# Weight sums tied in order to the score products, and spread over eight steps a group

## The chip, the cores and the metric

The kernel runs on one core of one Trainium2 chip. The metric is the device time of one execution in microseconds (us), lower is better. Engines: PE is TensorE, DVE is VectorE, ACT is ScalarE, POOL is GpSimd, and SP is the engine whose queue issues all the DMAs of this kernel.

## The reference

One decoder layer on 1024 tokens of width 1024. The normed input is projected; a gated linear recurrence with 4 heads and a causal attention with 8 heads of 64 run on parts of the projection; their outputs are merged by gates; then come a gated feed-forward network of width 2816 and a gated embedding. What matters here is the attention and the last product of the feed-forward network:

```python
s = jnp.einsum('bhtd,bhsd->bhts', qh[:, :, t0:t1], kh[:, :, :t1]) * scale
s = s + c[:, :, t0:t1, None] - c[:, :, None, :t1]
s = jnp.where(mask, s, -jnp.inf)
pr = jax.nn.softmax(s, axis=-1).astype(vh.dtype)
outs.append(jnp.einsum('bhts,bhsd->bhtd', pr, vh[:, :, :t1]))
...
x = x + (jax.nn.silu(hf @ w_ffn_gate[layer]) * (hf @ w_ffn_up[layer])) @ w_ffn_down[layer]
```

## The kernel before, in words

Every product of the projections is done as three products of numbers split into a high and a low part (`mm3`, lines 153 to 158, and lines 402 to 404 in `nproj`).

The last product of the feed-forward network is done by a scheme with seven block products instead of eight. It needs four sums of blocks of the weights for each of 11 pairs of row groups. These sums depend on nothing but the weights. `down_sums` (lines 775 to 794) makes them early, during the attention: for each pair, a "group", it loads four blocks of 128x512 (line 781), makes four sums in place on POOL (lines 783, 785, 788, 791) and stores each to DRAM (lines 786, 789, 792, 794), from where they are loaded much later. The tiles come from a pool of six buffers. `down_sums` is a generator, and each `next(wsums, None)` at line 870 runs one step of it, up to the next `yield`. A group takes five steps; the store of its last sum falls into the first step of the next group.

The attention runs in four passes, one for each pair of heads (`fox_mix`, line 847). A pass places the pair's q and k by DMA (`fox_place`, tiles QA, KA, QB, KB) and its values (`fox_values`, tiles VH, VL), and then has two parts. The first finds the largest score of each query: 24 products (line 862, for 16 of them with a mask product at line 865), each followed by a reduction on DVE (line 867), one step of the weight sums (line 870) and 0.6 step of other work (`fill(0.6)`). The maxima are transposed (line 875), split into uh and ul on DVE (lines 878, 879) and put by four DMAs into rows 66 and 67 of QA (line 882). The second part, the weighing, makes the scores again with these rows (lines 908, 909), takes the exponential on ACT (line 915), rounds it on POOL (line 919), makes the rest on DVE (line 920) and multiplies with the values (lines 896 to 898).

The work that `fill` takes is the stream of the pass: passes 0 and 1 have a projection of the attention (`fox_project`, 32 steps; it has a small power on POOL, line 661, and stores to DRAM, line 669) and two projections of gates (16 steps each, `gate_spill`, stored at line 684); pass 2 has three of the gates; pass 3 has one and three more that aren't stored. A pass fills 10 steps ahead of its first product, 14.4 beside the products, 5 ahead of the transposes and 9 behind them, and drains what is left at its end.

PE's order is that of the program (`manual_schedule`). The other engines' queues, SP's and POOL's among them, are ordered when the kernel is compiled: an instruction that the compiler takes to be ready can be put ahead of an earlier one that it takes not to be. Each queue then runs in that order, and waits where an operand isn't there yet.

Of the kernel before, what the change touches and what calls it, by code (L numbers as in the profile page):

```python
# [14 lines left out]
ALU = mybir.AluOpType  # L15
# [4 lines left out]
P = 128  # L20
# [3 lines left out]
HALF = 512  # L24
# [20 lines left out]
U_DOWN = U_UP + NFF  # L45
# [18 lines left out]
def layer(ctx, tc, xT, pT, wts, wf_in, consts, masks, outT):  # L64
    nc = tc.nc
    dma = nc.sync.dma_start
# [3 lines left out]
    ptt = nc.gpsimd.tensor_tensor  # L70
    pts = nc.gpsimd.tensor_scalar
    mm = nc.tensor.matmul
# [59 lines left out]
    order = [8, 9, 10, 11, 4, 0, 24, 25, 26, 27]  # L132
# [5 lines left out]
    for n, m in GATES_BEFORE:  # L138
        i = order.index(n)
# [145 lines left out]
    for c in range(8):  # L285
        t = w2() if c < 4 else hg.tile([P, HALF], F32, tag=("Kt", "Qt")[c % 2], name="vraw")
# [9 lines left out]
    identb = const.tile([P, P], BF, name="identb")  # L296
    nc.vector.tensor_copy(identb, ident)
    mnat = const.tile([P, P], BF, name="mnat")
# [394 lines left out]
    for i, (u, t) in enumerate(tiles):  # L693
        hi, lo = weight(u)
        for h in range(2):
            ps = zbank() if len(banks) < 3 else mbank()
# [60 lines left out]
    QA = [fx.tile([P, T], R, tag=f"QA{i}", bufs=1, name="QA") for i in range(2)]  # L757
    KA = [fx.tile([P, T], R, tag=f"KA{i}", bufs=1, name="KA") for i in range(2)]
# [12 lines left out]
    sd = dram.tile([4, NPAIR, P, HALF], F32, name="sd")  # L771
    wsum = fstack.enter_context(tc.tile_pool(name="wsum", bufs=6, reuse_waits="tile"))
    S2, S3, S4, S1 = range(4)

    def down_sums():

        for kp in range(NPAIR):
            t = {}
            for n, (i, b) in (("21", (0, 1)), ("22", (1, 1)), ("11", (0, 0)), ("12", (1, 0))):
                t[n] = wsum.tile([P, HALF], F32, tag="sw", name="sw")  # L780
                dma(t[n], wts[U_DOWN + 2 * kp + i][:, b * HALF:(b + 1) * HALF])
            yield
            ptt(t["22"], t["21"], t["22"], ALU.add)
            yield
            ptt(t["21"], t["11"], t["21"], ALU.subtract)
            dma(sd[S1, kp], t["22"])
            yield
            ptt(t["11"], t["22"], t["11"], ALU.subtract)
            dma(sd[S3, kp], t["21"])
            yield  # L790
            ptt(t["12"], t["12"], t["11"], ALU.subtract)
            dma(sd[S2, kp], t["11"])
            yield
            dma(sd[S4, kp], t["12"])

    wsums = down_sums()
    staged = {}

# [21 lines left out]
    def fox_place(pr):  # L820

        qhi, qlo = staged.pop((pr, 0))
        khi, klo = staged.pop((pr, 1))
        for a in range(2):
            s = slice(a * 64, a * 64 + 64)
            hd = pr * 2 + a
            dma(fb(QA[a][0:64]), fb(qhi[s]))
            dma(fb(KA[a][0:64]), fb(khi[s]))
            dma(fb(KA[a][64:65]), crow[hd:hd + 1])
            dma(fb(KA[a][65:66]), crow[8 + hd:9 + hd])  # L830
        for a in range(2):
            s = slice(a * 64, a * 64 + 64)
            dma(fb(QB[a][0:64]), fb(qlo[s]))
            dma(fb(QB[a][64:128]), fb(qhi[s]))
            dma(fb(KB[a][0:64]), fb(khi[s]))
            dma(fb(KB[a][64:128]), fb(klo[s]))
# [10 lines left out]
    def fox_mix(pr, steps, before):  # L847
        fox_place(pr)
        fox_values(pr)
        fill(10)  # L850

        u = const.tile([P, 16], F32, tag="u", name="u")
        u2 = const.tile([P, 8], F32, tag="u2", name="u2")
        for a in range(2):
            for b in range(8):
                tb = slice(b * P, (b + 1) * P)
                for g in range(1 if b < 4 else 2):
                    s1 = min((g + 1) * HALF, (b + 1) * P)
                    n = s1 - g * HALF
                    ps = mbank()  # L860
                    diag = s1 == (b + 1) * P and (b < 4 or g == 1)
                    mm(ps[:, 0:n], QA[a][0:66, tb], KA[a][0:66, g * HALF:s1], start=True,  # L862
                       stop=not diag)
                    if diag:
                        mm(ps[:, n - P:n], identb, mnat, start=False, stop=True)
                    dst = u[:, a * 8 + b:a * 8 + b + 1] if g == 0 else u2[:, a * 4 + b - 4:a * 4 + b - 3]
                    nc.vector.tensor_reduce(dst, ps[:, 0:n], axis=AX.X, op=ALU.max, negate=True)
                    if before:
                        before.pop(0)()
                    next(wsums, None)  # L870
                    fill(0.6)
            tt(u[:, a * 8 + 4:a * 8 + 8], u[:, a * 8 + 4:a * 8 + 8], u2[:, a * 4:a * 4 + 4], ALU.min)
        fill(5)
        pu = mbank()
        nc.tensor.transpose(pu[0:16, 0:P], u, ident)
        uh = fx.tile([16, P], R, tag="uh", bufs=1, name="uh")
        ul = fx.tile([16, P], R, tag="ul", bufs=1, name="ul")
        nc.vector.tensor_copy(uh, pu[0:16, 0:P])
        tt(ul, pu[0:16, 0:P], fb(uh), ALU.subtract)
        for a in range(2):  # L880
            for i, t in enumerate((uh, ul)):
                dma(fb(QA[a][66 + i:67 + i]), fb(t[a * 8:a * 8 + 8]))
        fill(9)
        LAG = 3
        HEAD = 0
        count = 0
        late = []
        for h in range(2):
            av = [abank(), abank()]
            nblk = 4 * (h + 1)  # L890
            pend = []

            def weigh():
                i, a, off, n, ph, pl = pend.pop(0)
                vs = slice(i * 192 + a * 64, i * 192 + a * 64 + P)
                mm(av[a][:, off:], VH[:, vs], ph[:, 0:n], start=i == 0, stop=False)
                mm(av[a][:, off:], VL[:, vs], ph[:, 0:n], start=False, stop=False)
                mm(av[a][:, off:], VH[:, vs], pl[:, 0:n], start=False, stop=i == nblk - 1)

            for i in range(nblk):  # L900
                t0 = max(i * P, h * HALF)
                t1 = (h + 1) * HALF
                n = t1 - t0
                sb = slice(i * P, (i + 1) * P)
                for a in range(2):
                    ps = mbank()
                    diag = i * P >= h * HALF
                    mm(ps[:, 0:n], KA[a][0:68, sb], QA[a][0:68, t0:t1], start=True, stop=False)  # L908
                    mm(ps[:, 0:n], KB[a][:, sb], QB[a][:, t0:t1], start=False, stop=not diag)
                    if diag:  # L910
                        mm(ps[:, 0:P], identb, mtr, start=False, stop=True)  # L911
                    p = fx.tile([P, HALF], F32, tag="p", bufs=2, name="p")
                    ph = fx.tile([P, HALF], R, tag="ph", bufs=3, name="ph")
                    pl = fx.tile([P, HALF], R, tag="pl", bufs=3, name="pl")
                    act(p[:, 0:n], ps[:, 0:n], AF.Exp)  # L915
                    if count < HEAD:
                        act(ph[:, 0:n], ps[:, 0:n], AF.Exp)
                    else:
                        pts(ph[:, 0:n], p[:, 0:n], 1.0, 0.0, ALU.mult, ALU.add)  # L919
                    tt(pl[:, 0:n], p[:, 0:n], fb(ph[:, 0:n]), ALU.subtract)  # L920
                    pend.append((i, a, t0 - h * HALF, n, ph, pl))
                    fill(0.87)
                    if len(pend) >= LAG:
                        weigh()
                    count += 1
                    if count in steps:
                        steps[count]()
                    if late and count % 2:
                        late.pop(0)()
            while pend:  # L930
                weigh()
                fill(0.87)
            den = f2()
            y = f2()
            nc.vector.tensor_copy(den[0:64], av[0][64:128])
            nc.vector.tensor_copy(den[64:128], av[1][0:64])
            nc.scalar.copy(y[0:64], av[0][0:64])
            nc.scalar.copy(y[64:128], av[1][64:128])

            def divide(q, h=h, den=den, y=y):  # L940
                s = slice(q * P, (q + 1) * P)
                nc.vector.reciprocal(den[:, s], den[:, s])
                tt(y[:, s], y[:, s], den[:, s], ALU.mult)
                if q == 3:
                    dma(yb[pr * P:(pr + 1) * P, h * HALF:(h + 1) * HALF], y)

            late += [lambda q=q, f=divide: f(q) for q in range(4)]
        return late
# [111 lines left out]
    op = ostack.enter_context(tc.tile_pool(name="op", bufs=3, side="right", reuse_waits="tile"))  # L1060
# [267 lines left out]
    for n, (p, kp) in enumerate(todo):  # L1328
# [22 lines left out]
        _, _, g, begin, into, done = products[p]  # L1351
# [129 lines left out]
```

## Time and profile before

| | us |
|---|---|
| median of 3 runs (lowest, highest) | 1703.51 (1701.68, 1705.78) |
| profiled execution | 1703.0 |
| its span | 1701.2 |
| PE busy | 1620.6 (95%) |
| DVE busy | 1097.1 (64%) |
| ACT busy | 639.1 (38%) |
| POOL busy | 600.0 (35%) |

The span runs from the first to the last instruction of the profiled execution; its own time has 1.8 us more. Busy is the time in which an engine executes; the rest of the span it waits or has nothing to do. The mean granted clock of PE is 0.98 of full.

### The profile page before, as it was taken

To read this page: it belongs to the slowest core of one execution; us is meant where nothing else is said; L and a number is where in the kernel's file an instruction comes from. 1 tells how busy PE (TensorE), PEld (TensorE's weight loads), DVE (VectorE), ACT (ScalarE), POOL (GpSimd) and SP (SyncE) were. 2 spreads that over 40 slices of the span, in tenths; PEclk is the share of its full clock that TensorE was granted. 3 is DMA by queue.
4 is the path that set the end of the run, shared out by engine and by line. 5 is a ranking of instruction groups with operands and counts; after the bars stand their busy time and mean duration, and the time that the engine had idled before them with its cause. 6 is when DMAs were issued, how large, how long until landed. Compare 5 with 4: busy or idle time off the path is not lost.

```text
span 1701.2 us, 21473 instructions
## 1 busy us (share of the span) xinstructions
PE 1620.6 (95%) x8086; PEld 1356.7 (80%) x8086; DVE 1097.1 (64%) x1431; ACT 639.1 (38%) x888; POOL 600.0 (35%) x452
## 2 busy tenths in 40 slices
PE   8999999998289799999999999999999999999998
PEld 7889889997168577777888888888888878888887
DVE  7457776755066566666557777777777757666442
ACT  7244645632032214357224433332333334444310
POOL 2343454423572503021213466566656620111200
PEclk9999999999599899999999999999999999999999
DMA  5332121245665653517134322233223278665111
GB/s 205 100 112 75 65 72 51 87 135 162 234 242 144 216 135 99 138 44 278 50 134 144 113 99 94 96 121 114 97 93 115 81 277 288 196 188 186 62 68 44
DMA packets 120615, 223.45 MB, mean 131 GB/s; under 512 B 14368, under 2 KB 43424, under 8 KB 120512
## 3 DMA queue, kind: packets, MB, share of 16 engines
q1 hardware_dynamic: 120512, 222.09, 39.7%
q8 instruction: 63, 1.03, 0.3%
q14 instruction: 40, 0.33, 0.1%
HBM read 148.25 MB, written 61.15 MB: 123 GB/s over the span
## 4 chain that ended last, share of the span: by engine, by line
PE 83%; issue 4%; POOL 3%; DMA 3%; DVE 3%; ACT 2%; SPq 1%; POOLq 0%; ACTq 0%; DVEq 0%
PE ps_z L156 14%; PE ps_z L157 14%; PE ps_z L158 14%; PE ps_m L156 6%; PE ps_m L158 6%; PE ps_m L157 6%; PE ps_z L402 2%; PE ps_z L403 2%; PE ps_z L404 2%; DMA sw<-wts 2%; PE ps_m L488 1%; PE ps_a L158 1%; PE ps_a L156 1%; PE ps_a L157 1%; PE ps_m L862 1%
## 5 line engine op out<-in xcount | busy, mean ns | idle before, releaser
L156 PE MATMUL ps_z<-xhi,whi 128*128 128x512 f32 x624 | 254.8, 408 | 0.2 <-ACT xhi L173 0.2
L157 PE MATMUL ps_z<-xlo,whi 128*128 128x512 f32 x624 | 246.0, 394 | 0.6 <-DVE xlo L176 0.5
L158 PE MATMUL ps_z<-xhi,wlo 128*128 128x512 f32 x624 | 245.3, 393 | 0.0
L158 PEld LDWEIGHTS ps_z<-xhi,wlo 128*128 128x128 f32 x624 | 118.3, 190 | 25.2
L1078 DVE TENSOR_TENSOR wlo<-dr,whi 128x1024 fp32r<-128x1024 f32 x75 | 94.9, 1267 | 66.6 <-ACT whi L1077 64.5
L157 PEld LDWEIGHTS ps_z<-xlo,whi 128*128 128x128 f32 x624 | 118.8, 190 | 23.0 <-DVE xlo L176 2.5
L156 PEld LDWEIGHTS ps_z<-xhi,whi 128*128 128x128 f32 x624 | 119.5, 192 | 21.6 <-ACT xhi L173 0.8
L128 ACT CAST whi<-raw 128x1024 fp32r<-128x1024 f32 (+1 forms) x69 | 72.4, 1049 | 169.7 <-PE ps_z L157 120.8
L920 DVE TENSOR_TENSOR pl<-p,ph 128x512 fp32r<-128x512 f32 (+3 forms) x96 | 62.6, 658 | 102.9 <-POOL ph L919 102.6
L1077 ACT CAST whi<-dr 128x1024 fp32r<-128x1024 f32 x75 | 79.1, 1055 | 108.6 <-PE ps_m L158 92.0
L129 DVE TENSOR_TENSOR wlo<-raw,whi 128x1024 fp32r<-128x1024 f32 (+1 forms) x69 | 100.6, 1458 | 29.0 <-ACT whi L128 24.6
L402 PE MATMUL ps_z<-whi,xhi 128*128 128x256 f32 (+1 forms) x384 | 112.8, 294 | 0.0
L919 POOL TENSOR_SCALAR ph<-p 128x512 fp32r<-128x512 f32 (+3 forms) x96 | 55.2, 578 | 157.7 <-ACT p L915 157.3
L403 PE MATMUL ps_z<-wlo,xhi 128*128 128x256 f32 (+1 forms) x384 | 108.6, 283 | 0.0
L404 PE MATMUL ps_z<-whi,xlo 128*128 128x256 f32 (+1 forms) x384 | 108.5, 283 | 0.0
L1271 POOL TENSOR_TENSOR w<-w,rb 128x512 f32<-128x512 f32 x44 | 63.1, 1435 | 103.4 <-ACT w L1270 103.4
L915 ACT ACTIVATE p<-ps_m 128x512 f32<-128x512 f32 (+3 forms) x96 | 46.2, 490 | 132.5 <-PE ps_m L911 92.6
L1300 POOL TENSOR_TENSOR acc<-acc,o 128x512 f32<-128x512 f32 x14 | 24.8, 1770 | 190.5 <-ACT o L1299 189.9
L908 PE MATMUL ps_m<-QA,KA 68*128 68x512 f32 (+3 forms) x96 | 35.0, 364 | 46.2 <-DMA QA<-ul 45.8
L403 PEld LDWEIGHTS ps_z<-wlo,xhi 128*128 128x128 f32 x384 | 73.3, 191 | 0.7
L402 PEld LDWEIGHTS ps_z<-whi,xhi 128*128 128x128 f32 x384 | 73.4, 191 | 0.1
L404 PEld LDWEIGHTS ps_z<-whi,xlo 128*128 128x128 f32 x384 | 73.0, 190 | 0.0
(465 smaller groups left out, 4454.2 us busy)
## 6 DMA issues: line engine op xcount, KB each, us to landing
raw<-wts SPq DMA_DIRECT2D x71, 512.0 KB
hb<-w SPq DMA_DIRECT2D x77, 256.0 KB
dr<-hb SPq DMA_DIRECT2D x75, 256.0 KB
sw<-wts SPq DMA_DIRECT2D x44, 256.0 KB
sd<-sw SPq DMA_DIRECT2D x44, 256.0 KB
rg<-wts SPq DMA_DIRECT2D x22, 512.0 KB
ru<-wts SPq DMA_DIRECT2D x22, 512.0 KB
dr<-sd SPq DMA_DIRECT2D x44, 256.0 KB
```

The lines of the kernel that those rows point to most:

```text
L128: nc.scalar.copy(hi, raw)
L129: tt(lo, raw, hi.bitcast(F32), ALU.subtract)
L156: mm(ps, w[0], x[0], start=first, stop=False, skip_group_check=more)
L157: mm(ps, w[0], x[1], start=False, stop=False, skip_group_check=more)
L158: mm(ps, w[1], x[0], start=False, stop=last, skip_group_check=more)
L402: mm(ps[:, off:off + n], xh[:, cs], hi, start=k == 0, stop=False)
L403: mm(ps[:, off:off + n], xh[:, cs], lo, start=False, stop=False)
L404: mm(ps[:, off:off + n], xl[:, cs], hi, start=False, stop=k == KT - 1)
L920: tt(pl[:, 0:n], p[:, 0:n], fb(ph[:, 0:n]), ALU.subtract)
L1077: nc.scalar.copy(hi, src)
L1078: tt(lo, src, hi.bitcast(F32), ALU.subtract)
L1271: ptt(s, s, hv(rb, h), ALU.mult)
```

## The change

Every load, sum and store of the weight sums gets an edge to the latest product of the largest scores (`anchor[0]`): it is put behind that product in the order made when the kernel is compiled. The edge is one of order alone (`NoSync`), and no wait comes from it. The steps of a group become eight: loads; two empty ones; a sum; then three times the store of the last sum and the next sum; then the last store. The sums and the order among them are the same.

```diff
+    anchor = [None]
+
+    def after_anchor(ins):
+
+        tc.add_manual_dep(ins.ins, anchor[0].ins.name,
+                          mybir.DependencyInfo(mybir.DependencyClass.NoSync,
+                                               mybir.DependencyReason.DATA), reason="order")
+
     def down_sums():
 
         for kp in range(NPAIR):
             t = {}
             for n, (i, b) in (("21", (0, 1)), ("22", (1, 1)), ("11", (0, 0)), ("12", (1, 0))):
                 t[n] = wsum.tile([P, HALF], F32, tag="sw", name="sw")
-                dma(t[n], wts[U_DOWN + 2 * kp + i][:, b * HALF:(b + 1) * HALF])
+                after_anchor(dma(t[n], wts[U_DOWN + 2 * kp + i][:, b * HALF:(b + 1) * HALF]))
             yield
-            ptt(t["22"], t["21"], t["22"], ALU.add)
             yield
-            ptt(t["21"], t["11"], t["21"], ALU.subtract)
-            dma(sd[S1, kp], t["22"])
             yield
-            ptt(t["11"], t["22"], t["11"], ALU.subtract)
-            dma(sd[S3, kp], t["21"])
+            for x, y, z, op, n in (("21", "22", "22", ALU.add, S1), ("11", "21", "21", ALU.subtract, S3),
+                                   ("22", "11", "11", ALU.subtract, S2), ("12", "11", "12", ALU.subtract, S4)):
+                after_anchor(ptt(t[z], t[x], t[y], op))
+                yield
+                after_anchor(dma(sd[n, kp], t[z]))
             yield
-            ptt(t["12"], t["12"], t["11"], ALU.subtract)
-            dma(sd[S2, kp], t["11"])
-            yield
-            dma(sd[S4, kp], t["12"])
...
-                    mm(ps[:, 0:n], QA[a][0:66, tb], KA[a][0:66, g * HALF:s1], start=True,
-                       stop=not diag)
+                    anchor[0] = mm(ps[:, 0:n], QA[a][0:66, tb], KA[a][0:66, g * HALF:s1],
+                                   start=True, stop=not diag)
                     if diag:
-                        mm(ps[:, n - P:n], identb, mnat, start=False, stop=True)
+                        anchor[0] = mm(ps[:, n - P:n], identb, mnat, start=False, stop=True)
```

## Rows read from the trace of the kernel before

**Rows 1.** The span in 40 slices of the page: PE's busy tenths and its granted clock.
```profile
PE   8999999998289799999999999999999999999998
PEclk9999999999599899999999999999999999999999
```

**Rows 2.** Windows cut at PE's marks: length, each engine's busy us, PEclk, DMA share, GB/s.
```profile
419.60:458.80 39.20, 0.02 (x1) 0.05 (x1) 0.84 (x2) 0.00 (x0) 23.18 (x19) 0.54 0.65 221
458.80:526.90 68.10, 59.15 (x293) 46.81 (x294) 42.07 (x55) 20.61 (x38) 35.72 (x39) 0.91 0.67 215
...
559.40:620.20 60.80, 55.86 (x263) 44.17 (x264) 36.15 (x57) 19.14 (x35) 21.27 (x30) 0.92 0.56 169
...
645.10:687.50 42.40, 42.13 (x220) 33.57 (x218) 30.41 (x52) 17.25 (x33) 14.51 (x24) 1.00 0.36 102
```

**Rows 3.** Timeline of PE: start us, us, operation, [idle before, what ended it].
```profile
458.78 0.77 PE L908 MATMUL ps_m<-QA,KA 68*128 68x512 f32 x1 [39.22 <-DMA QA<-ul]
...
463.67 0.43 PE L908 MATMUL ps_m<-QA,KA 68*128 68x384 f32 x1
...
559.39 0.77 PE L908 MATMUL ps_m<-QA,KA 68*128 68x512 f32 x1 [6.54 <-DMA QA<-ul]
...
562.85 0.47 PE L156 MATMUL ps_z<-xhi,whi 128*128 128x512 f32 x1
...
643.05 0.39 PE L156 MATMUL ps_z<-xhi,whi 128*128 128x512 f32 x1
...
643.73 0.39 PE L156 MATMUL ps_z<-xhi,whi 128*128 128x512 f32 x1
...
645.09 0.40 PE L908 MATMUL ps_m<-QA,KA 68*128 68x512 f32 x1
...
712.37 0.40 PE L908 MATMUL ps_m<-QA,KA 68*128 68x512 f32 x1
```

**Rows 4.** Timeline of DVE in pass 0.
```profile
416.56 0.28 DVE L879 TENSOR_TENSOR ul<-ps_m,uh 16x128 fp32r<-16x128 f32 x1
```

**Rows 5.** Timeline of SP's DMA queue, runs of one line merged.
```profile
400.29 2.46 SPq L781 DMA_DIRECT2D sw<-wts  x5
...
421.46 1.86 SPq L781 DMA_DIRECT2D sw<-wts  x4
...
440.06 1.88 SPq L781 DMA_DIRECT2D sw<-wts  x4
...
456.04 0.74 SPq L882 DMA_DIRECT2D QA<-uh  x1
...
626.90 0.43 SPq L844 DMA_DIRECT2D VL<-vfd  x1
...
628.53 9.48 SPq L684 DMA_DIRECT2D gd<-gst  x2
...
697.54 0.38 SPq L684 DMA_DIRECT2D gd<-gst  x1
```

**Rows 6.** The sums' tile, 393 to 460 us: duration ns min/median/max, first and last start.
```profile
L781 SPq DMA_DIRECT2D sw<-wts x20: 376/396/559, 400.3 to 450.2; - x20
...
L789 SPq DMA_DIRECT2D sd<-sw x5: 326/326/332, 417.5 to 455.6; - x5
...
L792 SPq DMA_DIRECT2D sd<-sw x4: 319/320/320, 419.7 to 447.5; - x4
```

**Rows 7.** Timeline of POOL.
```profile
412.89 1.64 POOL L661 TENSOR_TENSOR r<-ss,cf 128x8 f32<-128x8 f32 x1 [7.43 <-DVE ss L660]
...
425.06 1.26 POOL L783 TENSOR_TENSOR sw<-sw 128x512 f32<-128x512 f32 x1 [2.40 <-DMA sw<-wts]
...
583.59 2.33 POOL L791 TENSOR_TENSOR sw<-sw 128x512 f32<-128x512 f32 x1
```

**Rows 8.** The window of pass 0's weighing, the sums' tile alone: POOL busy (x), PEclk, DMA.
```profile
458.80:526.90 68.10, 20.83 (x15) 0.91 0.67 215
```

**Rows 9.** Timeline of PE in pass 0's weighing.
```profile
505.73 0.44 PE L896 MATMUL ps_a<-ph,VH 128*128 128x384 f32 x1 [1.64 <-POOL ph L919]
```

## The prediction

> **What bounds the kernel now.** I read the page's slices first [rows 1]. TensorE (PE) is busy in 90% or more of nearly every slice; the exceptions inside the run are slices 10 to 14, and in two of them, 11 and 14, the granted clock falls to a half and to eight tenths. A slice is 42.5 us, so whatever this change can give or take lies between about 380 and 600 us, or is taken from the passes behind. Elsewhere PE is full, and the change touches nothing there. These slices are the attention passes. I cut them at PE's own marks [rows 2]: the products of the largest scores with the fill after them (below: the max part), a gap, and the weighing up to the next pass's first such product. Gap 0 is 39.2 us with PE at next to nothing; gap 1, in pass 1, is 6.5 us [rows 3]. The weighing of pass 0 holds 59.15 us of PE in 68.1, that of pass 1 55.86 in 60.8, that of pass 2, in which no weight sum runs, 42.13 in 42.4.
>
> What ends the gaps is the same both times: the weighing's first product waits for the DMA that puts the maxima's low row into QA [rows 3]. The row itself was long there. In pass 0 VectorE had it at 416.8 [rows 4], while SP issued the DMA pair from 456.04 on [rows 5]. SP's queue shows what stood ahead: load after load of the sums, group after group at a pitch of 9.3 us (two groups from 421.46 to 440.06). Stores wait for GpSimd's additions and sit in the same queue as the QA rows. The counts [rows 6] say how much stood there: 20 loads, five second stores and only four third ones. With five steps a group, step 24 of the program, the last of pass 0, issues just the fifth group's second store. So here the queue is in program order: everything of the pass's 24 steps, then the maxima. The first group is slower, 21.2 us from load to next load, because its first addition stood behind a small power on GpSimd that began at 412.89 [rows 7]; a later one waits 3.6 us from load to addition.
>
> The weighing of pass 0 loses time in another way. Sums that belong to pass 1 run ahead into it, 15 additions of them [rows 8], between GpSimd's roundings of the weights, and PE waits for a rounded weight [rows 9].
>
> **What the change does, part by part.** It adds and removes no instruction and no byte: 44 loads, 44 additions, 44 stores. The ties are order without a wait, so none costs time by itself. Eight steps a group put three whole groups into each of passes 0 to 2 and two into pass 3 (24 steps a pass, 88 in all), where passes 0 and 1 had nearly all the work. What moves are 12 loads, 12 additions and 12 stores per pass, and what each is moved past counts on SP and on GpSimd. A tie holds a sum from running ahead of its product; it doesn't hold it from standing ahead of the QA rows. Since the queue of before is in program order at that place, I take it to be so after: each pass's groups first, then the maxima.
>
> Pass 0: three groups instead of almost five. The sequence up to the third group is that of now, so the QA rows go at 440.06, where the fourth group's loads are now, instead of 456.04: minus 16.0. The weighing starts 2.74 us after that issue, as now (456.04 to 458.78), so at 442.8, which is 49.1 us after the pass's first product.
>
> Weighing of pass 0: no sums. Its undisturbed length I take from pass 2: 42.4 us, plus the fill it has more. Passes 0 and 1 have 64 fill steps, pass 2 has 48, of three 512-column products each (0.68 us a step, 643.05 to 643.73 [rows 3]), so 16 x 0.68 = 10.9, and 0.3 for ten longer fill steps at its end: 53.6. It takes 68.1, so 14.5 is lost. Of this 2.4 is the restart: the first product takes 0.77 us where the same one takes 0.40 in pass 2, at the lower clock level (1.2 GHz for 2.4), and that lasts until 463.67, half of 4.9 us. The restart stays, since the gap does: minus 12.1.
>
> Pass 1: same fill, same powers on GpSimd as pass 0, now also three groups. Same offset of 49.1 from 526.9: weighing from 576.0 instead of 559.4, plus 16.6. Its restart lasts 3.4 us now (559.39 to 562.85), 1.7 lost; after a longer gap as in pass 0, plus 0.7. Weighing of pass 1: ideal 53.3, takes 60.8, of which 1.7 restart: minus 5.8.
>
> Pass 2: free of sums now. SP is free for the first load when the last part of VL is issued, at 627.3. No power is in the way, so three pitches of 9.3: QA rows at 655.2, weighing at 657.9 instead of 645.1: plus 12.8, and a restart between the two measured ones, plus 2.1. Pass 3: from 697.9, two pitches, weighing at 719.2 instead of 712.4: plus 6.8, restart 1.7. The fill covers only what lies before these starts, and that is already in the difference. The work queued behind the sums is the maxima's four DMAs, the next weight loads and a gate store; PE reaches none of them before the weighing starts.
>
> The sum: -16.0 - 12.1 + 16.6 + 0.7 - 5.8 + 12.8 + 2.1 + 6.8 + 1.7 = +6.8. The profiled execution took 1703.0 us (span 1701.2 and 1.8 around it), 0.5 under the median of the runs: forecast 1709.8.
>
> Bounds. No row shows an addition beside the maxima's reductions, which are what VectorE does in passes 2 and 3. The nearest rows are 1.26 us (VectorE idle) and 2.33 (beside the weights' subtractions) [rows 7]; I take 1.26, since most additions run after the reductions end, and the upper end adds 4 x 1.07 = 4.3 for one group in each of two passes, 8.6. The Trainium skill, GPSIMD Engine Reference, Key points, says that GpSimd shares its SBUF interfaces with VectorE and contends with VectorE instructions of two SBUF inputs. A reduction from PSUM is none, so by that rule the sum is 1709.8 and by the upper row 1718.4; the long row fits the rule, as a subtraction has two SBUF inputs. The pitch could shrink to its four additions and a store, 5.4 us, if loads ran a whole group ahead; six buffers hold one group and a half, so that is an end only: 3.9 x 7 = 27 less, 1683.
>
> **Rivals.** (B) The maxima go first in passes 2 and 3. In passes 0 and 1 two stores of the projected rows can fill SP's pauses; in 2 and 3 these are missing, and the order could slip the QA rows in ahead of the sums. Then 12.8 + 2.1 + 6.8 + 1.7 fall away: 1686.4, faster. It decides where the four QA DMAs stand ahead of a pass's second group of loads. For it: the queue is not in program order everywhere. Against: no row has a QA row ahead of a sum of its own pass. (C) The same in all passes: both gaps and both losses go, 39.2 + 6.5 + 2.4 + 1.7 + 12.1 + 5.8 = 67.7, so 1635.3; if the sums then run under the weighing, at the 12.1 that four groups cost there now, 11 groups cost 33: 1669. (D) A store of a gate, which waits for PE, stands between the sums in passes 2 and 3 and stops SP: two gate stores take SP 9.5 us now, nearly all of it such a wait [rows 5]; 8 us in each of the two passes would give 1726. It counts from the point where the gate's half is finished after the sums before it. (E) The ties have no effect and sums still run ahead: pass 0 gains 16.0, the weighing of pass 0 stays, gap 1 with its restart goes (8.2), the weighing of pass 1 gets as bad as that of pass 0 (6.3 more): 1685.
>
> **How the numbers follow.** Chances: forecast 0.56, B 0.17, C 0.10, D 0.12, E 0.05. No change means within 0.2%, 3.4 us, about what a measurement of this kernel can tell. The forecast's own spread is 1696 to 1722, since it is a difference of 33.9 us gained and 40.7 lost: 0.05 of it faster, 0.13 within, 0.38 slower. Faster: 0.05 + 0.17 + 0.10 + 0.05 = 0.37; same 0.13; slower 0.38 + 0.12 = 0.50. The range reaches down past B and E to the short pitch, and up almost to D; C and most of D are left out.
>
> **What would show it.** Right: four gaps in PE, about 23 us in passes 0 and 1, 13 in pass 2 and 7 in pass 3, each ended by the QA rows; 12 loads ahead of them in SP's queue; no sums and next to no PE idling in the weighings of passes 0 and 1 beyond the restart. Wrong: no gap in passes 2 and 3 (B), no gap anywhere (C), sums between the roundings again (E), or SP waiting at a gate store with additions done (D). A gap 0 still near 39 us would undo the first term.

## The result, and the profile after

The changed kernel takes 1719.89 us (median of 4 runs, 1719.14 to 1721.52) where the kernel before, on the same chip, takes 1704.64 (1701.68 to 1708.43): a ratio of 1.009 [1.0067, 1.0112], so it is slower by 0.9%, and the interval lies clear of 1. The forecast was 1709.8: the sign was right, the loss more than twice the one forecast. The profiled execution took 1719.1 us, 16.1 more than that of before; its span is 1717.4, the mean granted clock 0.975.

The page's slices of the changed kernel (busy tenths of PE, granted clock), to be held against [rows 1]:

```profile
PE   8999999997694969799999999999999999999998
PEclk9999999999796989899999999999999999999999
```

Before, the weakness lay in slices 10 to 14. Now it comes at intervals from slice 10 to slice 17: four holes instead of one deep and one shallow. PE's timeline shows them; every idle time of over 1 us between 395 and 745 us stands here:

```profile
443.01 0.80 PE L912 MATMUL ps_m<-QA,KA 68*128 68x512 f32 x1 [23.33 <-DMA QA<-ul]
...
547.32 0.77 PE L912 MATMUL ps_m<-QA,KA 68*128 68x512 f32 x1 [23.62 <-DMA QA<-ul]
...
646.69 0.77 PE L912 MATMUL ps_m<-QA,KA 68*128 68x512 f32 x1 [19.36 <-DMA QA<-ul]
...
727.11 0.77 PE L912 MATMUL ps_m<-QA,KA 68*128 68x512 f32 x1 [10.44 <-DMA QA<-ul]
```

All four end with the rows of the maxima (QA from ul), as the two of before did [rows 3]. The bracket is the idle time ahead of the weighing's first product. 39.2 and 6.5 us have become 23.3, 23.6, 19.4 and 10.4.

Next the windows, cut at the same marks as [rows 2] (a max part with its gap, a weighing, and so on; columns as there: length, then busy us of PE, PE's weight loads, DVE, ACT and POOL, then PE's granted clock, the DMA engines' busy share and GB/s):

```profile
393.80:443.00 49.20, 25.88 (x190) 23.12 (x188) 21.67 (x41) 7.01 (x12) 22.91 (x16) 0.80 0.57 179
443.00:497.80 54.80, 53.99 (x293) 44.93 (x294) 34.49 (x55) 20.37 (x38) 12.53 (x24) 0.96 0.44 127
497.80:547.30 49.50, 25.90 (x190) 23.14 (x189) 21.68 (x41) 5.72 (x11) 22.92 (x16) 0.78 0.63 191
547.30:602.30 55.00, 54.17 (x264) 43.78 (x264) 35.15 (x56) 19.22 (x35) 12.54 (x24) 0.95 0.46 134
602.30:646.70 44.40, 24.92 (x121) 18.57 (x119) 16.06 (x32) 1.05 (x1) 15.23 (x12) 0.83 0.70 220
646.70:691.60 44.90, 44.63 (x218) 35.22 (x219) 31.48 (x53) 18.18 (x34) 14.77 (x24) 0.94 0.39 115
691.60:727.10 35.50, 24.96 (x120) 18.56 (x119) 17.85 (x33) 4.54 (x5) 10.21 (x8) 0.90 0.74 219
```

The weighings of passes 0 and 1 are clean now: POOL, the fifth of the busy times, runs its 24 roundings and nothing else in pass 0 (12.53 us, against 35.72 and 39 instructions [rows 2]), and PE is busy in 53.99 of 54.8 us. What the two passes gain there, passes 2 and 3 lose ahead of their weighings.

Last, SP's queue, which sets the gaps (that it does is shown below, by `e3`). Columns: issue time, time taken, line, operation, how many merged. Pass 0 of the changed kernel, and pass 2 below it:

```profile
400.42 2.47 SPq L789 DMA_DIRECT2D sw<-wts  x5
...
421.57 1.87 SPq L789 DMA_DIRECT2D sw<-wts  x4
...
431.02 1.40 SPq L789 DMA_DIRECT2D sw<-wts  x3
...
440.35 0.75 SPq L886 DMA_DIRECT2D QA<-uh  x1
...
610.01 2.04 SPq L789 DMA_DIRECT2D sw<-wts  x4
...
617.55 4.84 SPq L797 DMA_DIRECT2D sd<-sw  x4
622.44 1.88 SPq L789 DMA_DIRECT2D sw<-wts  x4
624.38 0.42 SPq L684 DMA_DIRECT2D gd<-gst  x1
628.81 4.34 SPq L797 DMA_DIRECT2D sd<-sw  x4
633.20 1.88 SPq L789 DMA_DIRECT2D sw<-wts  x4
...
639.53 4.34 SPq L797 DMA_DIRECT2D sd<-sw  x4
643.96 0.71 SPq L886 DMA_DIRECT2D QA<-uh  x1
```

In both passes twelve loads go ahead of the QA rows. In pass 0 they come in runs of 5, 4 and 3: one load of the next group is always issued ahead. In pass 2 they come in runs of 4, 4 and 4: nothing is ahead, and every group's first addition waits for loads that SP issues only after the last store of the group before. GpSimd's timeline shows what that costs; two rows of pass 0, three of pass 2:

```profile
425.35 5.28 POOL L795 TENSOR_TENSOR sw<-sw 128x512 f32<-128x512 f32 x4 [2.57 <-DMA sw<-wts]
434.63 5.28 POOL L795 TENSOR_TENSOR sw<-sw 128x512 f32<-128x512 f32 x4 [3.99 <-DMA sw<-wts]
...
616.24 5.38 POOL L795 TENSOR_TENSOR sw<-sw 128x512 f32<-128x512 f32 x4 [25.12 <-DMA sw<-wts]
627.52 5.28 POOL L795 TENSOR_TENSOR sw<-sw 128x512 f32<-128x512 f32 x4 [5.90 <-DMA sw<-wts]
638.24 5.28 POOL L795 TENSOR_TENSOR sw<-sw 128x512 f32<-128x512 f32 x4 [5.44 <-DMA sw<-wts]
```

From the issue of a run of loads to the first addition it takes 3.8 and 3.6 us in pass 0 (421.57 to 425.35, 431.02 to 434.63), but 6.2, 5.1 and 5.0 in pass 2 (610.01 to 616.24, and so on). The four additions themselves take the same 5.3.

### The profile page after: what moved, and what is told of

It reads as the page before. It is cut to its first block, busy times and chain, and to the rows that moved or that the text cites. A ratio compares the mean times of both kernels' runs of the same rounds, so it can differ in the third digit from the quotient of the medians.

```text
span 1717.4 us, 21469 instructions
## 1 busy us (share of the span) xinstructions
PE 1618.3 (94%) x8086; PEld 1356.8 (79%) x8086; DVE 1088.9 (63%) x1431; ACT 638.7 (37%) x888; POOL 596.1 (35%) x452
## 4 chain that ended last, share of the span: by engine, by line
PE 85%; DMA 3%; POOL 3%; DVE 3%; issue 2%; ACT 2%; SPq 1%; POOLq 0%; DVEq 0%; ACTq 0%
PE ps_z L156 14%; PE ps_z L157 14%; PE ps_z L158 14%; PE ps_m L156 6%; PE ps_m L158 6%; PE ps_m L157 6%; POOL sw L795 3%; PE ps_z L402 2%; PE ps_z L403 2%; PE ps_z L404 2%; DMA sw<-wts 1%; PE ps_m L488 1%; PE ps_a L158 1%; PE ps_a L157 1%; PE ps_a L156 1%
## 5 line engine op out<-in xcount | busy, mean ns | idle before, releaser
L924 DVE TENSOR_TENSOR pl<-p,ph 128x512 fp32r<-128x512 f32 (+3 forms) x96 | 55.4, 583 | 130.7 <-POOL ph L923 130.2
L795 POOL TENSOR_TENSOR sw<-sw 128x512 f32<-128x512 f32 x44 | 58.3, 1324 | 81.4 <-DMA sw<-wts 78.8
L912 PEld LDWEIGHTS ps_m<-QA,KA 68*128 68x128 f32 x96 | 19.3, 201 | 82.3 <-DMA QA<-uh 54.6
```

Source lines behind the costliest of these rows:

```text
L795: after_anchor(ptt(t[z], t[x], t[y], op))
```

## The experiments

Each run was timed beside the kernel before on the same chip (medians of before: 1704.64 for the first four, 1703.64 for the next four, 1703.4 and 1703.8 for the last two pairs). None of these kernels leaves any of the computation out.

### The two halves of the change, each alone

**Ties with the old five steps** (`e1`), the changed kernel with its generator as before, every line of it tied:

```diff
-            for x, y, z, op, n in (("21", "22", "22", ALU.add, S1), ...
-                after_anchor(ptt(t[z], t[x], t[y], op))
-                yield
-                after_anchor(dma(sd[n, kp], t[z]))
+            after_anchor(ptt(t["22"], t["21"], t["22"], ALU.add))
+            yield
+            after_anchor(ptt(t["21"], t["11"], t["21"], ALU.subtract))
+            after_anchor(dma(sd[S1, kp], t["22"]))
...
```

> The ties alone, with five steps a group. Theory (time is set by how many groups stand ahead of the maxima's rows in SP's queue, times their pitch): pass 0 keeps its gap of 39 us, its weighing loses its sums (minus 13), pass 1 now has five groups ahead of its rows too (gap 39 to 40 instead of 6.5), its weighing is clean (minus 6), pass 2 has one group and a rest (2 to 5): about 1720 us, no better than the changed kernel. Rival (the ties are what helps, the spreading is what harms): below the kernel before, near 1690.

Measured: 1719.33 us, ratio 1.0086 [1.0071, 1.0101]. PE's timeline in this run:

```profile
458.91 0.76 PE L916 MATMUL ps_m<-QA,KA 68*128 68x512 f32 x1 [38.80 <-DMA QA<-ul]
...
579.81 0.76 PE L916 MATMUL ps_m<-QA,KA 68*128 68x512 f32 x1 [38.76 <-DMA QA<-ul]
```

Gap 0 is the old one. Pass 1 gets a gap of the same length, because the sums that used to run ahead into the weighing of pass 0 now wait for pass 1's own products. Pass 2 has a gap of 1.5 us, pass 3 none. The theory held, with the time within 1 us of the 1720 expected.

**Eight steps without the ties** (`e2`):

```diff
     def after_anchor(ins):
-        tc.add_manual_dep(ins.ins, anchor[0].ins.name, ...
+        return ins
```

> The eight steps alone, without ties. Theory: three groups ahead of the rows in pass 0 (gap 23 instead of 39), four run ahead into each of the weighings of passes 0 and 1 and cost what they cost in the weighing of pass 0 before (12 each), no gap in passes 1 to 3: 1703 - 16 - 8 + 6, about 1685 us. Rival (the spreading is what costs): as slow as the changed kernel, 1715 to 1720.

Measured: 1694.62 us, ratio 0.9945 [0.9929, 0.9962], faster than both kernels. PE's timeline in this run:

```profile
445.78 0.79 PE L910 MATMUL ps_m<-QA,KA 68*128 68x512 f32 x1 [23.52 <-DMA QA<-ul]
...
563.96 0.80 PE L898 MATMUL ps_a<-ph,VH 128*128 128x512 f32 x1 [6.67 <-POOL ph L921]
```

One gap is left, in pass 0. The sums run ahead again, and PE waits in the weighing of pass 1 for rounded weights (ph), and 3.2 us for zt (the next pair's q and k). That weighing is 75.6 us long (540.37 to 615.99), so the 1685 us expected were missed by 10. So the spread alone is worth 10.0 us against the before of its own runs, and the ties turn this gain into a loss of 15.2.

### The row order on SP

**The four DMAs of the maxima on ACT's queue** (`e3`), else as changed:

```diff
-                dma(fb(QA[a][66 + i:67 + i]), fb(t[a * 8:a * 8 + 8]))
+                nc.scalar.dma_start(fb(QA[a][66 + i:67 + i]), fb(t[a * 8:a * 8 + 8]))
```

> The changed kernel with the maxima's four DMAs issued from ACT's queue instead of SP's. If SP's queue alone holds the weighing back, all four gaps (77 us) and their restarts (8) go: about 1635 us. Rival: the additions that stand ahead of the first roundings in POOL's queue take the wait's place; then PE starts in time, does what doesn't need a rounded weight, and waits again until POOL has done two groups: 10 to 13 us gained per pass, 1670 to 1700 us. If neither queue matters: 1720.

Measured: 1682.24 us, ratio 0.9863 [0.9847, 0.988]. First PE's timeline, then GpSimd's in the same stretch:

```profile
430.94 0.79 PE L900 MATMUL ps_a<-ph,VH 128*128 128x512 f32 x1 [6.29 <-POOL ph L923]
...
...
425.01 5.29 POOL L795 TENSOR_TENSOR sw<-sw 128x512 f32<-128x512 f32 x4 [4.28 <-DMA sw<-wts]
430.26 1.20 POOL L923 TENSOR_SCALAR ph<-p 128x512 fp32r<-128x512 f32 x2
```

The four gaps are gone, but for 2.2 us in pass 1. So what held the weighing was the place of sixteen small DMAs in SP's order. The rival that GpSimd takes the wait's place held as well: the first roundings (430.26) stand behind a group's additions, and PE waits for them. The Trainium skill, Trainium Kernel Development and Optimization, Key Constraints, says that issuing DMAs from several engines at once saves only the sequencer's issue time. Those sixteen DMAs take SP about 2.9 us a pass (440.35 to 443.2 in pass 0), so an estimate by that rule, with no more than these issues counted, is some 11 us in all. The run shows 37.7 (1719.89 less 1682.24), and the measurement decides: what was saved is the wait in SP's queue, behind stores that wait for GpSimd.

### The size of the step in passes 2 and 3

**A lead of one load** (`e4`) and **of two** (`e5`): with a group's four loads goes the first one, or the first two, of the next group, so that the runs of loads in pass 2 needn't start from nothing. Else as changed:

```diff
+            for n, i, b in blocks:
+                load(kp, n, i, b)
+            for n, i, b in blocks[0:1]:
+                load(kp + 1, n, i, b)
```

(`blocks[0:2]` in the second; `load` allocates the tile and issues the tied DMA, once for each block.)

> The changed kernel with the first load of the next group issued together with a group's loads, so that passes 2 and 3 have the lead of one load that passes 0 and 1 have. Theory (the mis-sized term is the pitch without that lead, 10.8 us against 9.3): gap 2 shrinks from 19.4 to about 15.5, gap 3 from 10.4 to about 8, gaps 0 and 1 hardly change: 1712 to 1715 us. Rival (the longer pitch comes from gate stores and other transfers in passes 2 and 3): no change, 1720.

> The changed kernel with the first two loads of the next group issued together with a group's loads. Theory (time is groups times pitch, and the pitch is a load's way plus what is added and stored behind it): with both operands of the next group's first addition there already, only the second addition waits for a load, pitch about 8 us instead of 9.3 with one lead and 10.8 with none; gaps 2 and 3 about 14 and 6.5, gaps 0 and 1 about 20: 1698 to 1706 us. Rival (SP's or the DMA engines' throughput sets the pitch): as with one load of lead, 1711.

Measured: 1711.16 us, ratio 1.0034 [1.0021, 1.0048], and 1701.2, ratio 0.9975 [0.9965, 0.9986]. PE's gaps of passes 2 and 3 and pass 2's runs of loads in SP's queue, with a lead of one; then the same two gaps with a lead of two:

```profile
639.93 0.77 PE L921 MATMUL ps_m<-QA,KA 68*128 68x512 f32 x1 [16.08 <-DMA QA<-ul]
...
717.23 0.77 PE L921 MATMUL ps_m<-QA,KA 68*128 68x512 f32 x1 [7.81 <-DMA QA<-ul]
...
606.57 2.24 SPq L790 DMA_DIRECT2D sw<-wts  x4
...
618.15 2.81 SPq L790 DMA_DIRECT2D sw<-wts  x4
...
627.57 1.87 SPq L790 DMA_DIRECT2D sw<-wts  x4
```

```profile
636.44 0.80 PE L921 MATMUL ps_m<-QA,KA 68*128 68x512 f32 x1 [14.28 <-DMA QA<-ul]
...
712.75 0.76 PE L921 MATMUL ps_m<-QA,KA 68*128 68x512 f32 x1 [4.70 <-DMA QA<-ul]
```

With one load in front the pitch of the second group in pass 2 is 9.42 us (618.15 to 627.57), like pass 0's 9.45 in the change (421.57 to 431.02), where pass 2 of the change has 10.76 (622.44 to 633.20). The first group of pass 2 still takes 11.58 us (606.57 to 618.15), for 12.43 in the change. With the lead of one the time lies just under the 1712 to 1715 expected and 1.4 us above the prediction's forecast. Gaps 2 and 3 give 5.9 us of the 8.7 gained; another 2.2 come from gap 1, which fell from 23.62 to 21.44. The lead of two takes back the whole loss, within the 1698 to 1706 expected. This is the step that the prediction mis-sized.

### What stands behind the sums on the other engines

**The rounding on ACT too** (`e6`): the rows on ACT's queue, and ph by a second exponential on ACT, which `HEAD` switches on for all 24 blocks of a pass. **The same in the kernel before** (`e7`): five steps, no ties, both edits.

```diff
-        HEAD = 0
+        HEAD = 24
```

> The changed kernel with the maxima's DMAs on ACT's queue and, beside that, the rounded weights made by a second exponential on ACT, so that POOL has only the sums in the passes. Theory (the two holds are SP's queue ahead of the rows and POOL's queue ahead of the roundings; with both gone nothing that PE needs is behind a sum, but the next weight loads on SP): 1635 to 1655 us, no gap ended by POOL. Rival (ACT, with 24 more exponentials of 0.5 us in each pass, becomes the bound of the weighing): 1665 us or more, PE waiting for ACT.

> The kernel before (five steps, no ties) with the same two moves to ACT. Theory: the place of the sums matters only through what stands behind them, so the two ways of placing them come close to each other: 1640 to 1665 us, above the other by what the weight loads wait behind five groups in pass 0. Rival (the ties and the eight steps are worth something by themselves once the holds are gone): 15 us or more above it.

Measured: 1675.5 us, ratio 0.984 [0.9825, 0.9854], and 1677.54, ratio 0.9849 [0.9834, 0.9864]. With both edits the change and the kernel before differ by 2 us. But neither came below 1670, and both expected times failed (1635 to 1655 and 1640 to 1665). The rival of the first held in part: PE does wait for ACT in it, 5.90 us at most (at 631.94). But the longest wait was another. In the first of the two runs it reads, on PE, DVE and GpSimd (all in pass 0):

```profile
443.26 0.69 PE L902 MATMUL ps_a<-pl,VH 128*128 128x384 f32 x1 [12.06 <-DVE pl L924]
...
439.93 1.74 DVE L666 TENSOR_TENSOR zn<-zn,r 128x512 f32<-128x512 f32 x1 [10.71 <-POOL r L661]
...
435.68 2.60 POOL L795 TENSOR_TENSOR sw<-sw 128x512 f32<-128x512 f32 x2 [3.98 <-DMA sw<-wts]
438.24 1.65 POOL L661 TENSOR_TENSOR r<-ss,cf 128x8 f32<-128x8 f32 x1
```

From the top down: PE waits for the rest of the weights (pl), DVE has pl in its order behind zn, zn waits for the small power, and the power stands on GpSimd behind the first two of the third group's additions, which wait for their loads. A power of 1.65 us costs PE 12.

**The power on ACT as well** (`e9`), on top of the first of the two above; **the sums' DMAs on GpSimd's queue** (`e10`), on top of the same, with the power left on GpSimd:

```diff
-                    ptt(r16[:, hs], ss[:, hs], neghalf[:, 0:8], ALU.pow)
+                    act(r16[:, hs], ss[:, hs], AF.Ln)
+                    act(r16[:, hs], r16[:, hs], AF.Exp, scale=-0.5)
```

```diff
-                after_anchor(dma(t[n], wts[...]))
+                after_anchor(nc.gpsimd.dma_start(t[n], wts[...]))
...
-                after_anchor(dma(sd[n, kp], t[z]))
+                after_anchor(nc.gpsimd.dma_start(sd[n, kp], t[z]))
```

> The rows and the rounding on ACT as in the run with both, and the small power of the projection made on ACT as well (a logarithm and an exponential), so that GpSimd is left with the additions alone. Theory: what is left of the gap with both on ACT (a wait of 12.06 us for the rest of the weights, pl) comes from that power, which stands on GpSimd behind the third group's additions; DVE holds zn, and behind it pl, until it comes. Then that wait goes and the time falls by 10 to 16 us, to 1660 to 1666. Rival: the sums' hold comes back through the DMAs that still stand behind them on SP (weights, q and k), and the power has no part: within 4 us of 1675.5.

> The rows and the rounding on ACT as in the run with both, and the sums' loads and stores issued from GpSimd's own queue instead of SP's. Now nothing of the sums stands on SP. Rival to the power: if SP's order is the last hold, the weights, q and k come early and the time falls to 1640 to 1655. Theory: the power still stands behind the additions, which themselves now wait behind the issues on the same engine, so the long wait for pl stays at 10 us or more; 1668 to 1685.

Measured: 1661.53 us, ratio 0.9747 [0.973, 0.9764], and 1666.83, ratio 0.9777 [0.976, 0.9795]. Of PE's timeline with the power on ACT, the two longest waits left in the attention:

```profile
531.84 0.80 PE L901 MATMUL ps_a<-ph,VH 128*128 128x512 f32 x1 [3.76 <-ACT ph L922]
...
618.88 0.79 PE L901 MATMUL ps_a<-ph,VH 128*128 128x512 f32 x1 [5.52 <-ACT ph L922]
```

The wait of 12 us is gone and the time fell by 14.0, as the chain said. With the sums' DMAs on GpSimd the wait for pl is 8.79 us instead of 12.06, so neither side's numbers held to the letter: the theory's range began at 1668 and its wait at 10, the rival's range ended at 1655.

**All three on ACT in the kernel before** (`e11`), and **with the change, the power on ACT and the sums' DMAs on GpSimd** (`e12`); the edits are those shown above.

> The kernel before, its sums with five steps and no ties, with the rows, the rounding and the power on ACT: nothing that the pass waits for stands behind the sums on GpSimd, and the rows don't stand behind them on SP. Theory: the cost of the sums came from what stood behind them, so their placing has next to nothing left to decide: within 5 us of the same three with the change (1661.5), 1657 to 1667. Rival: placing still counts, and the sums that run ahead into the weighings of passes 0 and 1 cost there what they cost in the kernel before (12.1 and 5.8 us, less what passes 2 and 3 give back): 1670 or more.

> The change with the rows, the rounding and the power on ACT and the sums' loads and stores on GpSimd's queue: GpSimd and its queue hold the sums alone, and SP none of them. Theory: the two holds are separate, the power's (14.0 us gained by itself) and SP's (8.7 by itself), and add up in part: 1648 to 1658. Rival: they are the same waits, freed once: 1659 to 1664.

Measured: 1672.12 us, ratio 0.9815 [0.9793, 0.9836], and 1661.95, ratio 0.9746 [0.9721, 0.9772]. The second takes the time of the power alone, as its rival had it. That the two holds were the same waits, as the rival also had it, isn't shown: the two long waits for ACT above are gone, but pass 0, from its first product to that of pass 1, takes 98.4 us where it takes 83.1 with the power alone, and passes 1 and 2 take 2.3 and 7.5 less. In the first the rival's time held: with all three moved, the placing of the change is worth 10.6 us (1672.12 less 1661.53; the intervals of the ratios don't touch). The largest part of it is one wait. PE's row and SP's issue of that tile in the kernel before with all three; then SP's issue with the change (`e9`):

```profile
466.22 1.97 PE L816 MATMUL ps_m<-cf,zt 128*128 128x128 f32 x8 [10.65 <-DMA zt<-qd]
...
459.85 1.70 SPq L803 DMA_DIRECT2D zt<-qd  x2
```

```profile
442.37 1.62 SPq L807 DMA_DIRECT2D zt<-qd  x2
```

Without the change, pass 0 has nearly five groups, and the next pair's q and k (zt) stand behind them on SP, 17.5 us later. Pass 0 takes 96.7 us there and 83.1 with the change, 13.5 more; pass 1 takes 1.0 more, and pass 2, which has no sums there, 7.0 less. So the loss is a DMA behind the sums on SP, more than the rival's price of sums between the roundings.

### The sums after the attention

`e8` is the kernel before with the sums moved out of the attention into the stage that follows it, four steps of the generator for each half there, with five buffers, and with fewer of that stage's own tiles (`NY` 4 instead of 6) to make room:

```diff
-                    next(wsums, None)
                     fill(0.6)
...
+            for _ in range(4):
+                next(wsums, None)
```

> The kernel before with the weight sums taken out of the attention and made beside the products of the two branches (five buffers, four prefetched y tiles instead of six). Theory: the attention is rid of all it pays, 39 + 6.5 + 4 + 12 + 6 = 68 us; the branch products last 88 us, in which SP has 11 x 9.3 = 102 us of sums, so up to 25 us come back there: 1636 to 1665 us, no gap ended by the maxima's rows. Rival (the attention's gaps come from something else, and the sums only fill them): 1700 us or more.

Measured: 1680.85 us, ratio 0.9867 [0.9853, 0.9882]. The slices of PE:

```profile
PE   8999999999999999996899999999999999999998
```

Slices 10 to 18 are full: the last weighing starts at 642.89 instead of 712.37 [rows 3], so the sums cost the attention 69.5 us in the kernel before. The prediction had put that at 67.7 (rival C). Some 47 us of it (69.5 less 22.8, 1703.64 to 1680.85) are lost again behind, above all in slices 19 and 20, where up to 25 were expected; so the 1636 to 1665 us expected failed. How much of that is the sums and how much the smaller number of tiles wasn't told apart.

## Why the prediction was right in sign and short in size

Measured terms are differences of window lengths, those above against [rows 2] and [rows 3] (before, the first products of passes 0 and 3 start at 393.67 and 687.48):

| step of the prediction | forecast | measured |
|---|---|---|
| pass 0, weighing starts earlier | -16.0 | -15.9 (65.1 to 49.2) |
| weighing of pass 0 without sums | -12.1 | -13.3 (68.1 to 54.8) |
| pass 1, weighing starts later | +16.6 | +17.0 (32.5 to 49.5) |
| weighing of pass 1, its restart in it | -5.1 | -5.8 (60.8 to 55.0) |
| pass 2, weighing starts later | +12.8 | **+19.5** (24.9 to 44.4) |
| weighing of pass 2, restart | +2.1 | +2.5 (42.4 to 44.9) |
| pass 3, weighing starts later | +6.8 | **+10.6** (24.9 to 35.5) |
| the rest (restart of pass 3) | +1.7 | +1.5 |
| sum | +6.8 | +16.1 |

**What held.** The reading of the queue: every pass puts its groups on SP first and the QA rows after them, so spreading the sums shortens one gap and opens three. The QA rows went at 440.35, 0.3 us from the place foretold. Passes 0 and 1 came out within 1.2 us in each term, the restarts within 0.4. Rivals B and C fell with the gaps in all four passes, E with the weighings free of sums. D fell on SP's queue: the gate store between the sums of pass 2 (624.38) takes 0.42 us and waits for nothing.

**What failed** is the step "No power is in the way, so three pitches of 9.3": the mechanism held, and this term of the sum was too small. Worked out for pass 2: the first group takes 12.43 us from load to next load and the other two 10.76 each, 33.95 together where the step has 27.9; SP comes free 0.6 later after the pass's first product than assumed (7.7 for 7.1), for a gate store of 0.51 us stands ahead of the loads (609.46). Together 6.7. In pass 3 12.25 and 10.96 stand against 18.6, less 0.85 of earlier start: 3.8. These 10.5 us are more than the whole miss of 9.3; the rest is the weighings' small gains.

The pitch of 9.3 was read in pass 0, where each run of loads has one load ahead. The prediction had the runs of 5 and 4 in view [rows 5] and counted only the time between them. Two things make it longer in passes 2 and 3. One is the missing lead: with it given back by hand (`e4`), the later groups of pass 2 take 9.42 and 9.62 us, and the gaps go from 19.4 to 16.1 and from 10.4 to 7.8. So the missing lead is shown to be the cause of 5.9 of the 10.5 us.

The other is that a pass's first group is slower, with the lead too: 11.58 and 11.49 us in passes 2 and 3 of `e4`. In the change the DMA engines are nearly full from the first group's loads to its first addition, just behind the issue of the pass's own q, k and values, and less so at the second group. The windows of pass 2, columns as above (0.95 and 0.75 are the DMA share):

```profile
610.01:616.24 6.23, 6.11 (x31) 4.28 (x30) 6.01 (x13) 0.26 (x1) 0.00 (x0) 1.00 0.95 284
622.44:627.52 5.08, 4.90 (x22) 3.71 (x20) 0.73 (x2) 0.00 (x0) 0.00 (x0) 1.00 0.75 233
```

That those transfers slow the first loads is argued from this share; no run thinned them out. So it is in part luck that `e4` comes within 1.4 us of the forecast: its first groups are still slower than 9.3, and its gap 1 is shorter than the change's.

Why the lead goes missing stays open. A power on GpSimd ahead of the first addition isn't needed for it: in `e9` the power runs on ACT (with the rows and the roundings), the sums and their ties are as in the change, and the loads of pass 0 still come in runs of 5, 4 and 3 on SP's queue:

```profile
406.88 2.46 SPq L790 DMA_DIRECT2D sw<-wts  x5
...
418.69 6.61 SPq L790 DMA_DIRECT2D sw<-wts  x4
...
429.76 1.40 SPq L790 DMA_DIRECT2D sw<-wts  x3
```

**A bound that did its work.** The price of an addition beside the maxima's reductions was bounded by 1.26 and 2.33 us, and 1.26 taken. GpSimd's tile in pass 2, all twelve additions (shortest, median and longest in ns):

```profile
L795 POOL TENSOR_TENSOR sw<-sw x12: 1259/1262/1295, 616.2 to 642.3; 128x512 f32<-128x512 f32 x12
```

In pass 2 the reductions run until 618.6, so the first additions do lie beside them, at 1.295 at most. The Trainium skill, GPSIMD Engine Reference, Specifications, names VectorE instructions with two SBUF inputs, beside those in a 2-port mode, as the ones that contend with GpSimd. The trace agrees in that the additions beside reductions from PSUM took no longer. The upper end of 8.6 us was not needed; that it would have given 1718.4, close to the time measured, is chance. The miss was no price of an instruction but the pitch of the groups.

**Rival E** gave 1685 for sums that still run ahead. The kernel that is this case (`e2`) takes 1694.6: the weighing of pass 1 with four groups in it took 75.6 us, where E allowed 6.3 over 60.8, 67.1.

## What to carry to other kernels

A DMA queue in program order turns one waiting store into a wait for everything behind it; before moving background work about, list what stands behind it on each engine (here rows on SP, roundings and a small power on GpSimd), for moving that out was worth 31.7 us with the sums as before (1703.8 to 1672.1) and 58.4 with the change (1719.9 to 1661.5), while placing the sums alone was worth anything between a gain of 10 and a loss of 15. A pitch read in one place of a queue needn't hold in another: here 9.4 us became 10.8 without a load ahead, and 12.4 where other transfers ran as well, so count the runs of loads and what else is under way, not just the time between them. And a change that loses by itself can be right once the hold that it collides with is gone: tied and spread, the sums lose 15 us in the kernel as it was, and gain 10.6 with the other three edits in place.

## What the runs showed of the hardware

- Behind each gap PE starts at the lower of its two levels (1.2 GHz for 2.4): the first product of the weighing takes 0.77 to 0.80 us, where without a gap it takes 0.40 [rows 3], and the granted clock over the first 5 us of the four weighings of the change is 0.57, 0.50, 0.50 and 0.65. That is 2.2, 2.5, 2.5 and 1.8 us lost (estimated as 5 us times what the clock lacks to 1); the least stands behind the shortest gap, 10.4 us. The weighing of pass 2, which had no gap before, is 2.5 us longer.
- From the issue of a run of loads to the first addition it takes 3.6 and 3.8 us in pass 0 of the change, where one load of the group was issued ahead, and 5.0 and 5.1 in pass 2, where none was. For pass 2's first group, with the DMA engines busy at 0.95, it takes 6.2.
- A second exponential in place of a rounding, and a logarithm with an exponential in place of the power, raise ACT's busy time from 638.7 to 720.2 us. Some 37 us of this are 29 table loads of 1.28 us ahead of the logarithms and exponentials of the power (lines 661 and 662 of `e9`). PE gains all the same: ACT had 63% of the span free.
